# Attention with the values as the stationary operand, in two parts, and with weights that are divided before they move

## The chip, the cores and the metric

One core of a Trainium2 chip runs the whole program. The metric is device microseconds of one launch; lower is better. TensorE (PE) multiplies, VectorE (DVE), ScalarE (ACT) and GpSimd (POOL) do the rest, SyncE (SP) issues nearly all DMAs.

## The reference

Two blocks of two layers each work on 512 tokens of width 1024, in float32. Besides the attention there are a linear recurrence, cross-attention, two MLPs, a gated delta rule and two mixtures of experts; they stay as they are. The four attentions that the change rewrites are all of this form, with heads of 64 columns:

```python
for blk in range(s_len // BLOCK):          # blocks of 128 queries
    sc = einsum("bqhd,bkhd->bhqk", q[:, q0:q1], k[:, :q1]) * scale
    p = softmax(where(mask, sc + bias, -inf), axis=-1)
    outs.append(einsum("bhqk,bkhd->bqhd", p, v[:, :q1]))
```

- "fox" (`ab`, 8 heads, causal, a bias per head and key),
- "dilated" (`cd`, 8 heads, causal, a bias by distance),
- "sliding" (`cd`, 8 query heads on 2 key heads, a window of 128, and one sink logit per head that enters the denominator alone),
- "nsa" (16 heads, three branches whose outputs are added with a gate per head and branch: attention to 31 compressed blocks, and two causal attentions).

## The kernel before

The kernel is written with a tile framework: pools of buffers with a tag and a count (`BUFS`, `BANKS`), engines named by hand, and a scheduler that orders each engine's instructions when the program is built, by a simulated time and by program order as priority. So matmuls of a later projection stand between those of an attention, as filler. On the chip each engine then works in that fixed order. A later tile of a tag waits until an earlier one is released.

Precise products are made of rounded parts ("F32R"): `split` (L106) writes the rounded high part on ACT and the rest on DVE, and `mm3` (L148) adds three products.

The causal attentions run pair by pair (two heads, e = 0 and 1) through `j` in 8 steps: query block 3, 2, 1, 0, both heads of each. One step:

- `probs` (L289): two matmuls (three in fox) of `nk` = 512, 384, 256 or 128 columns into a bank "s"; DVE takes the minimum of the far columns (L301) and of the masked near ones (L302); ACT writes P = exp to SBUF, and the sum as `den` (L304).
- `pv` (L307): each 128 columns of P are transposed by PE into a bank "o" (L312), copied to SBUF as PT by `copy` (L776; ACT and DVE take turns, L781 and L783), and multiplied (L316) with PT as the stationary operand and 64 columns of the values as the moving one, both plain float32, into a bank "pt".

One head of a causal attention ("a unit" below: one head in one branch) so has 10 blocks of 128 keys: 10 transposes and 10 products. There are 8 units each in fox and dilated, 32 in nsa; sliding has 8 smaller ones, of 7 blocks. Per pair, `o_norm` (L318) divides by the sums on DVE, and `pair_out` (L326) transposes the result by four more matmuls (L332) and splits it into `ys`. In nsa (`branch` L1733, `compressed` L1696, `gated` L1767), the three branch outputs of a step `c` (8 steps, a pair each) are scaled and added in `acc` by DVE (L1777, L1775) and POOL (L1779), then go through `pair_out`.

The residual `hT` (4 tiles of tag "h") stays in SBUF through `ab` and `cd`. In nsa, four tiles of tag "y" hold the bias strips, `z` of `out_moe` (L1127, L1129) is of tag "h" in layer 1, and the first half of the output projection there (L1151) already runs in nsa's second half.

Of the kernel before, what the change touches and what calls it, by code (L numbers as in the profile page):

```python
# [18 lines left out]
S = 512  # L19
# [14 lines left out]
class Kern:  # L34
# [235 lines left out]
    def k_parts(self, y, name="K", tag="x"):  # L270


        nc = self.nc
        K, L = self.pair(name, tag, F32R), self.pair("KL", tag, F32R)
# [14 lines left out]
    def probs(self, qk, nk, strip, mn, den, extra=None, floor=None):  # L289
# [7 lines left out]
        P = self.t("P", tag="P")  # L297
# [6 lines left out]
        nc.scalar.activation(P[:, :nk], p[:, :nk], AF.Exp, bias=mn, scale=-1.0, accum_out=den)  # L304
        return P
# [12 lines left out]
    def o_norm(self, o, den, heads):  # L318
# [5 lines left out]
        return ob  # L324

# [38 lines left out]
    def ab(self):  # L364
# [8 lines left out]
        v = self.tiles("v", 4, "x")  # L373
# [5 lines left out]
        def ev_v(c, t, p):  # L379
            nc.scalar.activation(v[t][:, c * 256:(c + 1) * 256], p, AF.Copy, scale=rms()[0][:, t:t + 1])  # L380
# [47 lines left out]
        def attend(i):  # L428
            mn, den = self.small((128, 8), "mn"), self.small((128, 8), "den")
            o = self.psum("pt")  # L430
            for j in range(8):
                qb, e = NT - 1 - j // 2, j % 2
                h, nk, qs = 2 * i + e, (qb + 1) * 128, slice(qb * 128, (qb + 1) * 128)
                u = 8 * qb + h
                P = self.probs(self.qk(*parts[i], e, qs, slice(0, nk)), nk, self.fstrip, mn[:, j:j + 1], den[:, j:j + 1],
                               extra=(at[:, u:u + 1].to_broadcast([128, 128]), crh[:, :nk]))
                self.pv(o[:, j * 64:(j + 1) * 64], P, nk, [v[b][:, h * 64:(h + 1) * 64] for b in range(qb + 1)])
            ys[4 + i] = self.pair("y", "y", F32R)
            self.pair_out(self.o_norm(o, den, 8), ys[4 + i])
# [3 lines left out]
        for i in range(4):  # L443
# [6 lines left out]
            attend(i)  # L450
        ys[:4] = [self.rpair("y") for _ in range(4)]
# [71 lines left out]
    def cd(self):  # L523
        nc, V = self.nc, VCOL
        xs, rms = self.rms_prep(self.hT, V["cd_norm"])
        C, Sn = self.pair("CS")
# [12 lines left out]
        v = self.tiles("v", 4, "x")  # L539
        vd_ = self.t("vd")  # L540
        vd = [vd_[:, t * 128:(t + 1) * 128] for t in range(NT)]

        def ev_v(c, t, p):
            nc.scalar.activation(v[t][:, c * 256:(c + 1) * 256] if c < 2 else vd[t], p, AF.Copy, scale=rms()[0][:, t:t + 1])
# [18 lines left out]
        def dilated(i):  # L563
            mn, den = self.small((128, 8), "mn"), self.small((128, 8), "den")
            o = self.psum("pt")
            for j in range(8):
                qb, e = NT - 1 - j // 2, j % 2
                h, nk, qs = 2 * i + e, (qb + 1) * 128, slice(qb * 128, (qb + 1) * 128)
                P = self.probs(self.qk(qp[i], *kp[i], e, qs, slice(0, nk)), nk, self.dstrip[:, 512 - nk:],
                               mn[:, j:j + 1], den[:, j:j + 1])  # L570
                self.pv(o[:, j * 64:(j + 1) * 64], P, nk, [v[b][:, h * 64:(h + 1) * 64] for b in range(qb + 1)])
            self.pair_out(self.o_norm(o, den, 8), ys[i])

        def sliding(i):

            mn, den = self.small((128, 8), "mn"), self.small((128, 8), "den")
            o = self.psum("pt")
            for j in range(8):
                qb, e = NT - 1 - j // 2, j % 2
                h, k0, qs = i + 4 * e, max(0, qb - 1) * 128, slice(qb * 128, (qb + 1) * 128)  # L580
                nk = (qb + 1) * 128 - k0
                P = self.probs(self.qk(qp[4 + i], *kp[4], e, qs, slice(k0, k0 + nk)), nk, self.sstrip[:, 256 - nk:],
                               mn[:, j:j + 1], den[:, j:j + 1], floor=self.nsink[:, h:h + 1])
                self.pv(o[:, j * 64:(j + 1) * 64], P, nk,
                        [vd[k0 // 128 + b][:, e * 64:e * 64 + 64] for b in range(nk // 128)])
            x = self.small((128, 8), "es")
            sinks = self.nsink.rearrange("p (e i) -> p i e", e=2)[:, i]
            nc.vector.tensor_tensor(x.rearrange("p (t e) -> p t e", e=2), mn.rearrange("p (t e) -> p t e", e=2),
                                    sinks[:, None].to_broadcast([128, NT, 2]), op=OP.subtract)
            nc.scalar.activation(x, x, AF.Exp)  # L590
            nc.vector.tensor_tensor(den, den, x, op=OP.add)
            ys.append(self.rpair("y"))
            self.pair_out(self.o_norm(o, den, 8), ys[4 + i])
# [11 lines left out]
        for i in range(8):  # L605
# [5 lines left out]
            (dilated if i < 4 else sliding)(i % 4)  # L611
        for j in range(8):
# [605 lines left out]
    def ln_out(self, z, layer, out, y, ohT, w):  # L1218
# [9 lines left out]
        def add(t):  # L1228
# [11 lines left out]
            Rs[t] = self.T("R", "h" if layer == 0 else "y")  # L1240
# [64 lines left out]
    def moe(self, layer, lg, Rs, z, gain, parts):  # L1305
# [68 lines left out]
        oh = self.one_hot(0, pos3, iota, "h" if layer == 0 else "y")  # L1374
        begun = [self.gather(Rs, oh, r) for r in range(2)]
        space = self.all_space("h" if layer == 0 else "y")
# [45 lines left out]
        for i in range(0, 16, 2):  # L1422
# [4 lines left out]
            oh = self.one_hot(i + 2, pos3, iota, "h" if layer == 0 else "y")  # L1427
# [203 lines left out]
    def strips_load(self):  # L1631

        nc = self.nc
        st = [self.T("strip") for _ in range(4)]
        for i in range(4):
            src = self.skew[i][:]
            nc.sync.dma_start(st[i].rearrange("p (h n) -> p h n", h=4),
                              bass.AP(src.tensor, src.offset + 127, [[383, 128], [128 * 384, 4], [1, 256]]))
        self.strips = [st[h // 4][:, (h % 4) * 256:(h % 4 + 1) * 256] for h in range(16)]
        CB = self.T("CB")[:, :896]  # L1640
        nc.sync.dma_start(CB, self.cbd)
        self.CB = CB.rearrange("p (h i) -> p h i", h=16)

    def nsa(self):
# [3 lines left out]
        VV = [self.pair("vv", "x") for _ in range(2)]  # L1648
        wv = [list(wv(0)), list(wv(1, "x"))]
        for t in range(NT):  # L1650
            for c in range(2):
                self.lin_1(wv[c], t, xs, lambda p: self.copy(VV[t // 2][t % 2][:, c * 256:(c + 1) * 256], p))
# [21 lines left out]
        qp = [None] * 8  # L1674

        def proj_k(j):
# [3 lines left out]
            def ev(n, p):  # L1680
                kk[(n - 4) // 2] = self.k_parts(p, "K", "hx"[j])
# [4 lines left out]
        def proj_q(c):  # L1686
            def ev(n, p):
                qp[c] = self.q_parts(p, scale=-0.125)
            self.lin_f(w, [8 + c], xs, ev)
# [6 lines left out]
        def compressed(c):  # L1696
# [22 lines left out]
            return L_, r  # L1719

        def compressed_out(c, L, r, acc):
            pt = self.psum("o")
            for i in range(2):
                nc.tensor.transpose(pt[:, i * 128:(i + 1) * 128], L[:, i * 128:(i + 1) * 128], self.ident)
# [314 lines left out]
```

## Time and profile before

| | |
|---|---|
| median of 3 runs | 2849.57 us (2845.95 to 2852.29) |
| the profiled execution | 2845.23 us, of it the span 2843.4 us |
| fox, in the span | 125 to 200 us |
| dilated | 819 to 896 us |
| sliding | 896 to 995 us |
| nsa | 2278 to 2515 us |

The bounds of the four stages are those of their P and PT instructions, to a few microseconds; filler of the neighbours lies in them. A window's row gives, for each engine, the time in which it had an instruction under way. Matmuls overlap each other, so the price of one is read from the distance of starts in a dense run, not from its duration.

### The profile page before, as it was taken

To read this page: it belongs to the slowest core of one execution; us is meant where nothing else is said; L and a number is where in the kernel's file an instruction comes from. 1 tells how busy PE (TensorE), PEld (TensorE's weight loads), DVE (VectorE), ACT (ScalarE), POOL (GpSimd) and SP (SyncE) were. 2 spreads that over 40 slices of the span, in tenths; PEclk is the share of its full clock that TensorE was granted. 3 is DMA by queue.
4 is the path that set the end of the run, shared out by engine and by line. 5 is a ranking of instruction groups with operands and counts; after the bars stand their busy time and mean duration, and the time that the engine had idled before them with its cause. 6 is when DMAs were issued, how large, how long until landed. Compare 5 with 4: busy or idle time off the path is not lost. (4 is left out here: it accounts for less than half of the span.)

```text
span 2843.4 us, 40163 instructions
## 1 busy us (share of the span) xinstructions
PE 2695.0 (95%) x15128; PEld 2302.5 (81%) x15128; DVE 1769.7 (62%) x3583; ACT 1363.5 (48%) x2541; POOL 182.0 (6%) x185
## 2 busy tenths in 40 slices
PE   8999999999999999999999999979987999997995
PEld 6889888888888988888887888978776888896874
DVE  7675564444457655545446777668668377678767
ACT  5654442333356534422245444327774355535774
POOL 1101010000111010100001000000001011000001
PEclk9999999999999999999999999999998999998998
DMA  4314233333232421335333222327886211014885
GB/s 135 99 51 142 62 101 97 97 96 97 89 89 82 130 78 49 117 98 164 109 90 127 69 62 63 113 62 232 269 272 214 80 32 67 16 46 141 264 263 213
DMA packets 122535, 332.60 MB, mean 117 GB/s; under 512 B 21716, under 2 KB 37748, under 8 KB 122328
## 3 DMA queue, kind: packets, MB, share of 16 engines
q1 hardware_dynamic: 119896, 321.43, 36.1%
q0 software_dynamic: 2432, 8.46, 0.8%
q8 instruction: 124, 2.03, 0.3%
q14 instruction: 83, 0.68, 0.1%
HBM read 301.49 MB, written 28.02 MB: 116 GB/s over the span
## 5 line engine op out<-in xcount | busy, mean ns | idle before, releaser
L130 ACT ACTIVATE wh<-ws 128x1024 fp32r<-128x1024 f32 (+2 forms) x521 | 534.0, 1030 | 897.9 <-PE lin L152 599.5
L131 DVE TENSOR_TENSOR wl<-ws,wh 128x1024 fp32r<-128x1024 f32 (+2 forms) x521 | 617.0, 1191 | 221.6 <-ACT wh L130 220.6
L151 PE MATMUL lin<-xs,wh 128*128 128x512 f32 (+2 forms) x1080 | 429.0, 397 | 7.3 <-ACT xs L196 5.8
L152 PE MATMUL lin<-xs,wh 128*128 128x512 f32 (+2 forms) x1080 | 429.6, 398 | 2.5 <-DVE xs L197 2.5
L153 PE MATMUL lin<-xs,wl 128*128 128x512 f32 (+2 forms) x1080 | 428.6, 397 | 0.9 <-DVE wl L131 0.9
L151 PEld LDWEIGHTS lin<-xs,wh 128*128 128x128 f32 (+2 forms) x1080 | 203.3, 188 | 50.7 <-ACT xs L196 6.4
L152 PEld LDWEIGHTS lin<-xs,wh 128*128 128x128 f32 (+2 forms) x1080 | 203.2, 188 | 47.5 <-DVE xs L197 6.6
L153 PEld LDWEIGHTS lin<-xs,wl 128*128 128x128 f32 (+2 forms) x1080 | 203.3, 188 | 42.5 <-DVE wl L131 1.4
L346 DVE TENSOR_TENSOR h<-lin,h 128x512 f32<-128x512 f32 x112 | 77.4, 691 | 247.7 <-PE lin L153 247.5
L153 PE MATMUL lin<-sr,wl 128*128 128x512 f32 x512 | 199.3, 389 | 0.0
L152 PE MATMUL lin<-sr,wh 128*128 128x512 f32 x512 | 199.3, 389 | 0.0
L151 PE MATMUL lin<-sr,wh 128*128 128x512 f32 x512 | 199.2, 389 | 0.0
L733 DVE SCALAR_TENSOR_TENSOR ra<-lin,bc 128x512 f32<-128x512 f32 x64 | 44.2, 691 | 168.5 <-PE lin L153 165.9
L1535 PE MATMUL o<-oh,Rl 128*128 128x256 f32 x512 | 132.6, 290 | 7.2 <-PEq L1378 7.2
L304 ACT ACTIVATE P<-s,mn 128x256 f32<-128x256 f32 (+1 forms) x224 | 114.2, 514 | 52.7 <-DVE mn L302 50.0
L1535 PE MATMUL o<-oh,Rh 128*128 128x256 f32 x512 | 133.7, 293 | 4.9 <-issue 2.2
L152 PE MATMUL s<-wl,exh 128*128 128x512 f32 x256 | 107.4, 420 | 13.1 <-DVE wl L131 13.1
L151 PE MATMUL s<-wh,exh 128*128 128x512 f32 x256 | 103.0, 405 | 10.1 <-ACT wh L130 10.0
L152 PEld LDWEIGHTS lin<-sr,wh 128*128 128x128 f32 x512 | 96.1, 188 | 20.0
L151 PEld LDWEIGHTS lin<-sr,wh 128*128 128x128 f32 x512 | 96.1, 188 | 20.0
L153 PEld LDWEIGHTS lin<-sr,wl 128*128 128x128 f32 x512 | 96.1, 188 | 19.8
L1535 PEld LDWEIGHTS o<-oh,Rl 128*128 128x128 f32 x512 | 101.3, 198 | 13.3 <-issue 10.1
(605 smaller groups left out, 6178.4 us busy)
## 6 DMA issues: line engine op xcount, KB each, us to landing
ws<-in_moe_wgu SPq DMA_DIRECT2D x128, 512.0 KB, 4.9
ws<-in_mlp_wu SPq DMA_DIRECT2D x64, 512.0 KB, 3.6
ws<-in_mlp_wd SPq DMA_DIRECT2D x64, 512.0 KB, 3.6
ws<-in_moe_wd SPq DMA_DIRECT2D x64, 512.0 KB, 5.5
yd<-ey SPq DMA_DIRECT2D x56, 256.0 KB, 2.8
ws<-in_gdn_w SPq DMA_DIRECT2D x24, 512.0 KB, 3.6
ws<-in_ab_w SPq DMA_DIRECT2D x16, 512.0 KB, 4.3
ws<-in_xa_wk SPq DMA_DIRECT2D x16, 512.0 KB, 3.7
```

The lines of the kernel that those rows point to most:

```text
L130: nc.scalar.activation(wh, ws, AF.Copy)
L131: nc.vector.tensor_tensor(wl, ws, rd(wh), op=OP.subtract)
L151: mm(out, a[0], b[0], start=start, stop=False)
L152: mm(out, a[0], b[1], start=False, stop=False)
L153: mm(out, a[1], b[0], start=False, stop=stop)
L304: nc.scalar.activation(P[:, :nk], p[:, :nk], AF.Exp, bias=mn, scale=-1.0, accum_out=den)
L346: self.nc.vector.tensor_tensor(self.hT[n], p, self.hT[n], op=OP.add)
L733: nc.vector.scalar_tensor_tensor(a, p, 0.0, rms()[1], op0=OP.max, op1=OP.mult)
L1535: self.nc.tensor.matmul(p[:, j * 256:(j + 1) * 256], Rs[t][i][:, fs], oh[:, t], start=t + i == 0, stop=t == NT - 1 and i == 1)
```

## The change

1. The values are kept in two rounded parts side by side, 64 columns high and 64 low (`v_parts`: one ACT and one DVE instruction per evacuation instead of one on ACT). They take tiles "h" (fox, dilated), so `hT` is given up: it is loaded again from `xT` after fox; in `cd` it is stored to DRAM at the start and loaded after dilated.
2. `weigh`: the query blocks go two at a time, (2, 3), then (1, 0). One DVE reciprocal of two sums, then POOL multiplies each P by 1/sum and by a second scalar (ones, or nsa's gate), in SBUF. The two long P share a tile of 1024 columns.
3. `turn`: the transposes as before; their result is split (ACT and DVE, both) into two parts PT; for the long blocks these take tiles "wh" and "wl", which weights use too.
4. `causal`: the values (high and low columns) are the stationary operand, PT the moving one, 256 or 128 columns wide. 12 matmuls of a unit go into one bank "pt" (e = 0) or "lin" (e = 1). Its upper and lower 64 rows are added once (`head_out`: ACT copy, DVE add). The output is already transposed, so `pair_out` falls away.
5. In nsa all three branches add up in that bank, so `gated` falls away. The bias strips are loaded per step into "bc"; `z` and `Rs` of layer 1 change tags ("y" and "h").
6. Sliding: the sink logit is put as one more column behind the scores (a small ACT copy), in place of the three instructions on `es`.

```diff
-        nc.scalar.activation(P[:, :nk], p[:, :nk], AF.Exp, bias=mn, scale=-1.0, accum_out=den)
-        return P
+        n = nk
+        if sink is not None:
+            n += 1
+            nc.scalar.activation(p[:, nk:n], sink, AF.Copy)
+        nc.scalar.activation(P[:, :n], p[:, :n], AF.Exp, bias=mn, scale=-1.0, accum_out=den)
+        return P[:, :nk]
...
+    def weigh(self, qbs, probs, gate, tag):
+        wide = tag != "P"
+        x, den = self.t("P", tag=tag, cols=1024 if wide else 512), self.small((128, 2), "den")
+        Ps = [probs(qb, x[:, j * 512:] if wide else x[:, j * 257:], den[:, j:j + 1]) for j, qb in enumerate(qbs)]
+        r = self.small((128, 2), "rd")
+        self.nc.vector.reciprocal(r, den)
+        for j, P in enumerate(Ps):
+            self.nc.gpsimd.tensor_scalar(P, P, r[:, j:j + 1], gate(qbs[j]), op0=OP.mult, op1=OP.mult)
+        return Ps
+    def turn(self, Ps, PT):
+        p, n = self.psum("o"), 0
+        for P in Ps:
+            for b in range(P.shape[1] // 128):
+                self.nc.tensor.transpose(p[:, n * 128:(n + 1) * 128], P[:, b * 128:(b + 1) * 128], self.ident)
+                n += 1
+        self.split(p[:, :n * 128], *(x[:, :n * 128] for x in PT))
+    def causal(self, o, probs, V, gate, tag, first=True, last=True):
+        mm = self.nc.tensor.matmul
+        PT = self.turned()
+        for j, P in enumerate(self.weigh((2, 3), probs, gate, tag)):
+            self.turn([P], [x[:, j * 512:(j + 1) * 512] for x in PT])
+        for k, i in ((0, 0), (1, 0), (1, 1), (3, 0), (3, 1), (2, 0), (2, 1), (0, 1)):
+            x = PT[i].rearrange("p (q c) -> p q c", q=2)[:, k // 3:, k * 128:(k + 1) * 128]
+            mm(o[:, 256 + k // 3 * 128:], V(k), x, start=first and k + i == 0, stop=False)
+        PT = [self.t("PT", F32R, "PT") for _ in range(2)]
+        self.turn(self.weigh((1, 0), probs, gate, "P")[::-1], PT)
+        for k, i in ((0, 0), (1, 0), (1, 1), (0, 1)):
+            mm(o[:, k * 128:256], V(k), PT[i][:, k * 256:256 + k * 128], start=False, stop=last and (k, i) == (0, 1))
+    def head_out(self, e, o, y):
+        u = self.t("oh")[:64]
+        self.nc.scalar.activation(u, o[64:], AF.Copy)
+        self.nc.vector.tensor_tensor(y[e * 64:e * 64 + 64], o[:64], u, op=OP.add)
...
-        z = [self.T("z", "y" if layer == 0 else "h") for _ in range(NT)]
+        z = [self.T("z", "y") for _ in range(NT)]
...
         for c in range(8):
-            acc = self.t("acc", tag="bc")
-            L, r = compressed(c)
-            branch(c, 0, acc)
...
+            y = self.t("ob")
+            for e in range(2):
+                o = self.psum(("pt", "lin")[e])
+                nc.tensor.matmul(o, BD[:, c // 4 * 2 + e], PT, start=True, stop=False)
+                for br in range(2):
+                    branch(c, br, e, o)
+                    if c < 7 and e == 0:
+                        if br:
+                            PTn = compressed(c + 1)
+                        else:
+                            if c == 3:
+                                proj_k(1)
+                            proj_q(c + 1)
+                self.head_out(e, o, y)
```

## Rows read from the trace of the kernel before

**Rows 1.** The page, part 1: busy time of each engine over the span.
```profile
PE 2695.0 (95%) x15128; PEld 2302.5 (81%) x15128; DVE 1769.7 (62%) x3583; ACT 1363.5 (48%) x2541; POOL 182.0 (6%) x185
```

**Rows 2.** Busy time by windows: fox, dilated, sliding, nsa (us, engines, clock, DMA).
```profile
125.00:200.00 75.00, 70.05 (x455) 61.12 (x454) 57.75 (x168) 48.60 (x123) 8.76 (x11) 0.98 0.14 40
819.00:896.00 77.00, 76.75 (x480) 66.52 (x480) 57.04 (x131) 52.06 (x122) 15.51 (x14) 1.00 0.27 73
896.00:995.00 99.00, 95.25 (x701) 88.41 (x700) 68.25 (x160) 56.40 (x138) 3.83 (x3) 0.97 0.40 120
2278.00:2515.00 237.00, 228.53 (x1659) 206.04 (x1658) 172.43 (x582) 132.25 (x374) 24.98 (x42) 0.99 0.11 37
```

**Rows 3.** Waits of PE in nsa: total us, times, longest.
```profile
PE o L312 <- ACT P L304: 5.3, 3, 3.1
```

**Rows 4.** Matmuls by line: records, ns min/median/max, first and last start.
```profile
L316 PE MATMUL pt<-vv,PT x640: 217/275/422, 2282.9 to 2511.9; 128*128 128x64 f32 x160
L316 PE MATMUL pt<-v,PT x320: 217/275/324, 132.2 to 895.5; 128*128 128x64 f32 x160
...
L316 PE MATMUL pt<-vd,PT x112: 217/275/475, 899.0 to 992.6; 128*128 128x64 f32 x112
...
L332 PE MATMUL o<-c_ident,ob x48: 270/273/421, 143.2 to 994.2; 128*128 128x128 f32 x48
```

**Rows 5.** Timeline of PE in fox: start us, merged us, line, tile, columns, count.
```profile
165.16 0.61 PE L332 MATMUL o<-c_ident,ob 128*128 128x128 f32 x4
...
182.05 2.67 PE L316 MATMUL pt<-v,PT 128*128 128x64 f32 x22
...
187.03 0.27 PE L296 MATMUL s<-KL,Q 128*128 128x128 f32 x1
187.14 0.27 PE L296 MATMUL s<-crh,at 128*128 128x128 f32 x1
...
190.36 0.28 PE L151 MATMUL lin<-mx,wh 128*128 128x256 f32 x1
190.48 0.28 PE L152 MATMUL lin<-mx,wh 128*128 128x256 f32 x1
```

**Rows 6.** Groups by line in nsa, DVE then ACT: busy us, mean ns of one.
```profile
L1775 DVE SCALAR_TENSOR_TENSOR acc<-pt,rg,acc 128x64 f32<-128x64 f32 x64 | 13.0, 276 | 2.1 <-PE pt L316 2.0
...
L783 DVE COPY PT<-o 128x512 f32<-128x512 f32 x16 | 11.0, 687 | 3.9 <-PE o L312 3.8
...
L783 DVE COPY PT<-o 128x384 f32<-128x384 f32 x16 | 8.9, 557 | 13.9 <-PE o L312 13.8
...
L783 DVE COPY PT<-o 128x256 f32<-128x256 f32 x16 | 6.8, 424 | 14.0 <-PE o L312 12.6 <-PE s L296 1.2
...
L1777 DVE TENSOR_TENSOR acc<-pt,rg 128x512 f32<-128x512 f32 x8 | 5.5, 691 | 0.9 <-PE pt L316 0.4
...
L783 DVE COPY PT<-o 128x128 f32<-128x128 f32 x16 | 4.6, 289 | 5.2 <-PE o L312 4.9
...
L1745 DVE RECIPROCAL rg<-den 128x8 f32<-128x8 f32 x16 | 3.2, 201 | 5.4 <-ACT P L304 5.2
...
L781 ACT ACTIVATE PT<-o 128x512 f32<-128x512 f32 x16 | 9.6, 597 | 2.8 <-PE o L312 2.5
```

**Rows 7.** Groups of POOL by line, whole span: busy us, mean ns of one.
```profile
L206 POOL TENSOR_TENSOR ssq<-ssq,sq 128x512 f32<-128x512 f32 x42 | 69.2, 1649 | 110.1 <-ACT sq L201 90.7 <-issue 19.2
...
L277 POOL MEMSET KL<- 64x512 f32 x26 | 13.5, 520 | 116.9 <-PE pt L1818 90.6 <-PE s L296 25.1
...
L1779 POOL TENSOR_TENSOR acc<-acc,gtmp 128x512 f32<-128x512 f32 x8 | 10.2, 1280 | 114.0 <-DVE gtmp L1777 114.0
```

**Rows 8.** Timeline of PE at the end of fox: two waits of transposes.
```profile
175.64 0.66 PE L312 MATMUL o<-c_ident,P 128*128 128x128 f32 x4 [1.81 <-ACT P L304]
...
177.83 1.01 PE L312 MATMUL o<-c_ident,P 128*128 128x128 f32 x4 [1.01 <-ACT P L304]
```

**Rows 9.** Timeline of SP in nsa: the last two loads of z.
```profile
2391.01 0.79 SPq L1129 DMA_DIRECT2D z<-rdram  x2
```

More of the change, by code (lines that the diff above doesn't have):

```diff
@@ L273, in k_parts @@
         nc = self.nc
-        K, L = self.pair(name, tag, F32R), self.pair("KL", tag, F32R)
+        K, L = self.pair(name, tag[0], F32R), self.pair("KL", tag[-1], F32R)
         for e in range(2):
@@ new lines, in turn, with turned @@
+    def turn(self, Ps, PT):
[5 more added lines that the diff above has]
+        self.split(p[:, :n * 128], *(x[:, :n * 128] for x in PT))
+    def turned(self):
+        self.uid += 1
+        return [self.wp.tile([128, 1024], F32R, tag=tag, name=f"PT{tag}_{self.uid}", bufs=BUFS[tag]) for tag in ("wh", "wl")]
@@ L372, in ab @@
         u, g = self.tiles("u", 4), []
-        v = self.tiles("v", 4, "x")
+        v = [self.T("v", "h", F32R) for _ in range(NT)]
         def ev(n, p):
@@ L450, in ab @@
             attend(i)
+        self.hT = self.tiles("h", 8, "h")
+        for k in range(8):
+            nc.sync.dma_start(self.hT[k], A["xT"][k])
         ys[:4] = [self.rpair("y") for _ in range(4)]
@@ L525, in cd @@
         xs, rms = self.rms_prep(self.hT, V["cd_norm"])
+        hd = self.dp.tile([1024, S], F32, tag="hd", name="hd")
+        for k in range(8):
+            nc.sync.dma_start(hd[k * 128:(k + 1) * 128], self.hT[k])
         C, Sn = self.pair("CS")
@@ L572, in dilated @@
-            self.pair_out(self.o_norm(o, den, 8), ys[i])
-        def sliding(i):
[L576 to L591, printed above, removed]
@@ new lines, in dilated, with probs @@
+            y = self.t("ob")
+            for e in range(2):
+                h, o = 2 * i + e, self.psum(("pt", "lin")[e])
+                def probs(qb, P, den):
+                    nk = (qb + 1) * 128
+                    return self.probs(self.qk(qp[i], *kp[i], e, slice(nk - 128, nk), slice(0, nk)), nk,
+                                      self.dstrip[:, 512 - nk:], self.small((128, 1), "mn"), den, P=P[:, :nk])
+                self.causal(o, probs, lambda b: v[b][:, h * 128:(h + 1) * 128], lambda qb: self.ones[:, 0:1], "y")
+                self.head_out(e, o, y)
@@ L592, in sliding @@
             ys.append(self.rpair("y"))
-            self.pair_out(self.o_norm(o, den, 8), ys[4 + i])
+            self.split(y, *ys[4 + i])
         def proj(i):
@@ L611, in cd @@
             (dilated if i < 4 else sliding)(i % 4)
+            if i == 3:
+                self.hT = self.tiles("h", 8, "h")
+                for k in range(8):
+                    nc.sync.dma_start(self.hT[k], hd[k * 128:(k + 1) * 128])
         for j in range(8):
@@ L1718, in compressed @@
             nc.gpsimd.tensor_tensor(r8(r), r8(r), gates(c, 0), op=OP.mult)
[L1719 to L1724, printed above, removed]
-            PT = self.t("PTc", tag="PT")[:, :256]
-            self.copy(PT, pt[:, :256])
-            o = self.psum("pt")
-            for i in range(NT):
-                nc.tensor.matmul(o[:, i * 128:(i + 1) * 128], PT[:, i // 2 * 128:(i // 2 + 1) * 128],
-                                 BD[:, i % 2, c // 4 * 128:(c // 4 + 1) * 128], start=True, stop=True)
-            self.gated(acc, o, r, False)
```

171 lines of the change are left out of this document (91 added, 80 removed).

## The prediction

> **What bounds the kernel now.** I read the page's busy shares first: TensorE is under way in 95% of the span [rows 1], so a saving must be matmul time or a gap between matmuls. Then the windows of the four stages that the change touches, 488 us together [rows 2]: PE is busy 70.05 of 75, 76.75 of 77, 95.25 of 99 and 228.53 of 237 us, DVE only 0.77, 0.74, 0.69 and 0.73 of the time, ACT less. In nsa, the longest, PE's largest wait is 5.3 us in total [rows 3]. So PE bounds these stages, and the projections that lie in them as filler keep it full. Where filler runs out it shows: at the end of fox, transposes wait 1.81 and 1.01 us for the exponentials [rows 8].
>
> Next, what a matmul costs, by the distance of starts in dense runs [rows 5]. 22 records of the product P·V start over 2.67 − 0.28 us, 0.114 us each. Their number is the point of the change: 640 + 320 + 112 = 1072 records [rows 4], while the code has 10 products per causal unit (48 units) and 7 per sliding unit (8 units), 536 in all. A float32 product thus runs as two records, 0.228 us for 64 columns. Products of rounded parts are one record each: 0.12 us for 256 columns (190.36 to 190.48), 0.11 for 128 (187.03 to 187.14). Transposes start (0.61 − 0.27)/3 = 0.113 us apart.
>
> **The change, part by part.**
>
> *PE.* A causal unit pays 20 × 0.114 = 2.28 us for P·V now. After, it has 8 matmuls of 256 columns and 4 of 128: 8 × 0.12 + 4 × 0.11 = 1.40. That is −0.88, times 48 = −42.2 us. A sliding unit: 14 × 0.114 = 1.60 against 6 × 0.12 + 2 × 0.11 = 0.94, times 8 = −5.3. `pair_out` goes: 20 pairs of 4 transposes (48 of the 80 in [rows 4]), 80 × 0.113 = −9.0. In nsa's compressed branch 2 transposes and 8 records become 4 transposes and two matmuls of 512 columns (twice the 256-column price): 1.14 to 0.93 per step, times 8 = −1.7. Scores and transposes of P stay. The sum is −58 us: fox −8.8, dilated −8.8, sliding −7.1, nsa −33.5.
>
> *DVE.* A unit's four copies of PT are shared with ACT now: (687 + 557 + 424 + 289)/2 = 0.98 us on DVE [rows 6]. After, each goes through both engines, in three pieces of 512, 384 and 384 columns: 0.687 + 2 × 0.557 = 1.80. Two reciprocals at 0.20 come on top: +1.22 us per unit. A pair gains two adds of `head_out` at 0.69 (as a 512-column copy) and loses the product of `o_norm` (0.69, as L1777) and one reciprocal. Fox and dilated: 2 × 1.22 + 1.38 − 0.89 = +2.9 per pair, +11.7 us per stage. Sliding, by the same prices with pieces of 512 and 384 columns and without the `es` steps: +1.8 per pair, +7. Nsa, per step: 4 × 1.22 + 1.38 + some 0.5 for the compressed split, less 1.62 (L1775, 13.0 us in eight steps), two products of L1777 (1.38) and four small steps (0.8): +3.0, +24 us. DVE then carries 69.4 us in fox, 68.7 in dilated, 75.5 in sliding, 196 in nsa, where PE alone would leave 66, 68, 92 and 204. So DVE is late next, in fox and dilated at once. *ACT* gains about as much per unit (0.6 for 512 columns, [rows 6]), but starts from 132 of 237 in nsa, and stays below DVE. The second part of the values costs DVE a step per evacuation in the projections, beside PE's work; nothing for that, at most 1 us where it delays a bank.
>
> *The waits added.* Between exponential and transpose there are now a reciprocal (0.20) and POOL's scaling. No row shows POOL with one tensor and two scalars. The nearest: a memset, 0.52 us for 512 columns, and two tensors of 512 columns, 1.28 and 1.65 [rows 7]. I take 0.9, nearer the memset as one tensor is read; bounds 0.5 and 1.65. Behind a copy there is now ACT and then DVE (+0.6). A phase (two query blocks) so gains 1.8 to 4 us of latency, hidden while other phases or filler feed PE. POOL's throughput is no bound: 1280 columns in four units of a step cost 5 to 16.5 us against some 26.
>
> The Trainium skill speaks against this choice: "GPSIMD Engine Reference", section "Engine selection", sends elementwise work on a tile to VectorE, since GpSimd is about twice as slow with two inputs, though near line rate with one. The trace agrees on two inputs (1.28 us against DVE's 0.69); with one, no row shows it. By the slow reading the latency takes its upper end, by the other its lower; the PE sum is the same.
>
> *Moved loads.* `hT` comes back by eight loads after fox and after dilated; `ab_wo` needs it only after the cross-attention's key and value projections, `cd_wo` after sliding: hidden. The stores in `cd` end during the first projection. On SP they queue behind the release of the values' tiles, and weights stand behind them; four weight buffers cover that, 0 to 5 us, taken as 1. In nsa `z` was loaded by 2391 us [rows 9], 120 us ahead of the end, so half of the output projection could be filler. After, `z` shares tag "y" with PT's sources, values' keys and `ys`, and its four loads must wait for the last units: the filler goes, and the end of the stage drains bare. Fox loses filler too, since "lin" and "wh"/"wl" now also serve attention. I price an uncovered end like the waits of [rows 8], 2.8 us, three times, +1 for the loads: +9 us in total, bounds 2 and 20.
>
> *The sum.* If PE stayed the bound: −58 + 9. If DVE is, a stage takes its DVE time over the share that DVE can be kept busy. The trace has 0.77 as the highest share here (DVE not the bound) and 0.96 for PE (the bound, nsa). I take 0.92, nearer the latter, since the engine that bounds is the one kept fed: fox 69.4/0.92 = 75.4 (0), dilated 74.7 (−2), nsa 213 (−24), sliding by PE 92 (−7). That is −33 + 9 = −24 us. The profiled execution took 2845.2 us, 4 us below the median of the runs; the forecast is for the median, so 2849.6 − 24 = 2826.
>
> **The rivals.**
>
> 1. *DVE cannot be fed* (slower). Every step of a phase crosses engines, and DVE works in a fixed order. With a share f the causal stages take 334/f, sliding 92, the ends 9; with f = 0.86 that is the old 488 us. So below 0.86 the kernel gets slower; at 0.82 it is 407 + 92 + 9 − 488 = +20: 2870. For it: 0.77 is the most these stages show. Against: it was never the bound there, and PE reaches 0.96.
> 2. *POOL's latency takes the gain* (no change). 112 phases that each leave PE idle 0.2 to 0.3 us cost 24 to 34 us: about 2850. For it: POOL prices at two inputs, and only two or three buffers for P and PT. Against: nsa has three "s" banks and filler in seven of eight steps.
> 3. *PE stays the bound throughout*: −58 + 9, 2800; at the lower bound of the ends 2793. For it: DVE durations overlap in part, so its sums are too high.
> 4. *The products still run as two records*. Then only 11 us of PE are saved and DVE's load remains: about 2865. Rows of rounded parts show single records [rows 5], so hardly.
>
> **How the numbers follow.** My forecast with 3 as its lower edge (2797 to 2841): 0.66. Rival 1: 0.21; rival 2: 0.10; rival 4: 0.03. The range of 8 in 10 goes from 2797 to 2866, up to the milder half of rival 1. A difference of 0.2% (5.7 us) is about what a measurement of this kernel can tell from no change. Faster: 0.66 and 0.04 of rival 2, 0.70. Same: 0.08 with the rest of rival 2 and the edge of rival 1. Slower: 0.22.
>
> **What would show it.** Right: the P·V matmuls of the three stages number 12 and 8 per unit, single records 0.11 to 0.12 us apart; L332's transposes are gone; nsa is some 15 to 30 us shorter with DVE's share at 0.85 or more; fox and dilated hardly change; PE's waits in nsa name DVE, POOL or ACT, and the last step drains longer. Wrong: a DVE share in nsa that stays near 0.75 with PE's share falling (rivals 1 and 2: which engine PE waits for tells them apart, and POOL's duration at 512 columns whether it is POOL), or a long gap behind nsa or ahead of `ab_wo` or `cd_wo`, where a load came late.

## The result, and the profile after

| | before | after |
|---|---|---|
| median (4 runs each) | 2849.53 us | 2993.06 us (2986.13 to 2994.28) |
| ratio, 95% interval | | 1.0501 (1.0481 to 1.0521) |
| span of the profiled execution | 2843.4 us | 2990.9 us |

The change costs 5%. The page of the kernel after, part 1 (busy time, share of the span, instructions; before in [rows 1]):

```profile
PE 2745.8 (92%) x14584; PEld 2312.5 (77%) x14584; DVE 1831.2 (61%) x3671; ACT 1432.9 (48%) x2677; POOL 320.8 (11%) x409
```

TensorE issues fewer matmuls, 14584 for 15128, and is busy longer. The windows of fox, dilated, sliding, nsa, and of the output projection behind nsa, which answer to [rows 2] (columns as there: length, PE, PEld, DVE, ACT, POOL busy, granted clock, DMA):

```profile
126.00:214.00 88.00, 69.46 (x351) 55.55 (x352) 58.97 (x174) 52.01 (x126) 26.58 (x41) 0.87 0.08 25
844.00:947.00 103.00, 80.03 (x360) 63.99 (x359) 61.95 (x146) 56.70 (x127) 36.29 (x44) 0.81 0.18 49
950.00:1073.00 123.00, 105.33 (x642) 93.86 (x641) 74.59 (x165) 67.41 (x172) 23.82 (x36) 0.83 0.38 114
2353.00:2646.00 293.00, 242.48 (x1267) 197.47 (x1268) 187.71 (x580) 161.55 (x425) 98.00 (x171) 0.87 0.10 30
2647.00:2707.00 60.00, 57.98 (x469) 56.50 (x468) 39.62 (x102) 18.32 (x21) 0.53 (x6) 0.98 0.30 97
```

The four windows last 607 us; those of [rows 2] last 488. No engine is full: PE is under way in 0.83 of nsa, DVE in 0.64. Before, PE was idle in 8.5 us of nsa, now in 50.5. And the granted clock, 0.97 to 1.00 in the four windows before, is 0.81 to 0.87: PE now spends a part of each stage at the lower of its two levels, 1.2 instead of 2.4 GHz; in nsa the granted 0.87 means the lower level for 0.26 of 293 us, some 76 us, for some 5 before. PE's largest waits in nsa (for [rows 3]), and two waits of ACT and DVE there (us in total, times, longest):

```profile
PE s L296 <- ACT P L307: 22.2, 25, 2.8
PE o L1812 <- DVE Lp L108: 7.7, 8, 1.2
PE o L348 <- POOL P L340: 4.5, 9, 2.1
ACT Q L263 <- PE lin L153: 27.0, 7, 6.5
DVE Q L267 <- ACT Q L263: 28.6, 7, 6.5
```

PE waits most for a score bank that an exponential still holds, hardly for GpSimd. ACT and DVE stand 27 and 28.6 us behind seven query projections, where before they waited 0.4 and 0.3 us. A part of one step of nsa shows how it looks, first as four windows:

```profile
2429.50:2433.50 4.00, 3.18 (x24) 2.61 (x22) 1.83 (x4) 1.52 (x3) 0.00 (x0) 1.00 0.00 0
2433.50:2436.40 2.90, 0.14 (x1) 0.00 (x0) 1.38 (x2) 1.95 (x5) 0.00 (x0) 1.00 0.00 0
2437.00:2443.00 6.00, 5.68 (x28) 4.50 (x29) 3.70 (x13) 4.26 (x12) 2.41 (x4) 0.72 0.01 4
2443.00:2449.00 6.00, 6.00 (x30) 4.66 (x29) 1.89 (x8) 1.25 (x6) 2.41 (x4) 1.00 0.29 89
```

PE's instructions around the gap in it (timeline: start, length, idle time before and what ended it):

```profile
2432.79 0.85 PE L370 MATMUL lin<-PT,vv 128*128 128x128 f32 x3
2436.40 0.33 PE L296 MATMUL s<-K,Q 128*128 128x128 f32 x1 [2.76 <-ACT P L307]
2436.57 0.28 PE L296 MATMUL s<-KL,Q 128*128 128x128 f32 x1
...
2438.19 1.87 PE L348 MATMUL o<-c_ident,P 128*128 128x128 f32 x7
```

A head's last products end, and PE stands 2.76 us until an exponential frees a bank. The clock falls. The next head's chains start at half speed (28 matmuls in 6 us). Then the whole query projection, 24 matmuls, runs in one block with only two products of attention in it, at full clock, while ACT and DVE do little. A gap need not be that long: four of the twelve falls of the clock in nsa come behind a gap of 2.76 us, most of the others behind several of 0.4 to 0.8 us each (at 2420.2 us, for one, behind 0.40, 0.83, 0.36 and 0.60).

Call an unbroken run of projection matmuls in PE's order a group. By the trace, those of nsa stand in 78 groups before and in 17 after, the longest of 68; in fox 21 groups become 3, in dilated 38 become 9. Before, they filled the attention's gaps; after, attention and projection take turns.

**What the prediction counted, in the trace.** Products of nsa for one output bank (groups by form: duration min/median/max in ns, first and last start), for [rows 4]:

```profile
L366 PE MATMUL pt<-PTwh,vv x64: 220/330/522, 2365.7 to 2635.7; 128*128 128x256 f32 x48, 128*128 128x128 f32 x16
L370 PE MATMUL pt<-PT,vv x64: 221/283/337, 2367.6 to 2636.7; 128*128 128x256 f32 x32, 128*128 128x128 f32 x32
```

Starts in a dense run of them (timeline), for [rows 5]:

```profile
2431.87 0.39 PE L366 MATMUL lin<-PTwl,vv 128*128 128x256 f32 x1
2432.09 0.23 PE L366 MATMUL lin<-PTwh,vv 128*128 128x128 f32 x1
2432.15 0.27 PE L366 MATMUL lin<-PTwl,vv 128*128 128x128 f32 x1
2432.26 0.33 PE L366 MATMUL lin<-PTwh,vv 128*128 128x256 f32 x1
2432.43 0.40 PE L366 MATMUL lin<-PTwl,vv 128*128 128x256 f32 x2
2432.67 0.97 PE L370 MATMUL lin<-PT,vv 128*128 128x256 f32 x4
```

With the low parts and the other bank that is 12 single records per unit, 384 in nsa for 640. L332's transposes are gone.

### The profile page after: what moved, and what is told of

The parts are those of the page before. It is cut to its first block, busy times and chain, and to the rows that moved or that the text cites. A ratio compares the mean times of both kernels' runs of the same rounds, so it can differ in the third digit from the quotient of the medians.

```text
span 2990.9 us, 39635 instructions
## 1 busy us (share of the span) xinstructions
PE 2745.8 (92%) x14584; PEld 2312.5 (77%) x14584; DVE 1831.2 (61%) x3671; ACT 1432.9 (48%) x2677; POOL 320.8 (11%) x409
## 5 line engine op out<-in xcount | busy, mean ns | idle before, releaser
L296 PE MATMUL s<-K,Q 128*128 128x384 f32 (+1 forms) x224 | 94.2, 422 | 53.1 <-ACT P L307 47.2
L307 ACT ACTIVATE P<-s,mn 128x384 f32<-128x384 f32 (+1 forms) x224 | 114.3, 514 | 54.0 <-DVE mn L301 34.3
L348 PE MATMUL o<-c_ident,P 128*128 128x128 f32 x536 | 108.7, 337 | 29.1 <-POOL P L340 28.1
L348 PEld LDWEIGHTS o<-c_ident,P 128*128 128x128 f32 x536 | 77.0, 171 | 51.4 <-POOL P L340 43.5
L151 PEld LDWEIGHTS lin<-sr,wh 128*128 128x128 f32 x512 | 96.1, 188 | 20.0
```

What stands on the lines that cost most here:

```text
L151: mm(out, a[0], b[0], start=start, stop=False)
L296: nc.tensor.matmul(p[:, :nk], q, k, start=i == 0, stop=i == len(qk) - 1)
L307: nc.scalar.activation(P[:, :n], p[:, :n], AF.Exp, bias=mn, scale=-1.0, accum_out=den)
L348: self.nc.tensor.transpose(p[:, n * 128:(n + 1) * 128], P[:, b * 128:(b + 1) * 128], self.ident)
```

## Experiments

To read a stage alike in all kernels I take its time from its first minimum step on VectorE to the next event: fox to the first residual add of its output projection, dilated to sliding's first minimum, sliding to the first residual add of its output projection, nsa to the last matmul of its output projection. The kernel before, run beside them, took 2847.06 (e1 to e4), 2857.76 (e5 to e8), 2854.09 (e9 to e12), 2853.61 (e13 to e16), 2852.89 and 2851.76 us. Each changed kernel below was run once, so a difference of some 10 us means nothing. Each edit is also scheduled anew, so the order of every engine's instructions can change with it. Only e16 has the order of the kernel before in all engines; e7, e13 and e14, which add one or two instructions to it, do not.

| kernel | total | fox | dilated | sliding | nsa | sum of four |
|---|---|---|---|---|---|---|
| before | 2849.5 | 123 | 77 | 101 | 281 | 582 |
| after | 2993.1 | 151 | 107 | 134 | 354 | 746 |
| e1 scaling on VectorE | 2995.6 | 149 | 106 | 132 | 365 | 752 |
| e2 no division | (4383.7) | 142 | 94 | 128 | 341 | 705 |
| e3 long blocks one by one | 2987.4 | 144 | 107 | 144 | 344 | 739 |
| e4 lin free | 2988.3 | 153 | 104 | 134 | 356 | 747 |
| e5 scores ahead | 2992.7 | 151 | 103 | 138 | 354 | 746 |
| e6 fill | 3138.1 | 166 | 116 | 142 | 465 | 889 |
| e8 heads in turn | 3063.5 | 159 | 116 | 132 | 413 | 820 |
| e9 weights early | 2987.1 | 150 | 107 | 137 | 351 | 745 |
| e10 one copy | 2972.0 | 148 | 103 | 131 | 343 | 725 |
| e11 four weight buffers | 3192.0 | 158 | 100 | 135 | 353 | 746 |
| e15 chain as before | 2960.3 | 137 | 95 | 128 | 353 | 713 |
| e17 block products | 3036.1 | 150 | 109 | 124 | 399 | 782 |
| e18 filler free | 2920.1 | 136 | 94 | 124 | 315 | 669 |
| *on the kernel before:* e7 division | 2937.0 | 138 | 86 | 100 | 349 | 673 |
| e12 two weight buffers | 2893.1 | 130 | 79 | 103 | 287 | 599 |
| e13 GpSimd's step alone | 2875.9 | 129 | 91 | 99 | 298 | 617 |
| e14 reciprocal alone | 2894.8 | 131 | 79 | 100 | 321 | 631 |
| e16 single-part products | 2813.4 | 118 | 74 | 99 | 258 | 549 |

### One part of the change undone at a time: e1 to e5

```diff
e1  -  self.nc.gpsimd.tensor_scalar(P, P, r[:, j:j + 1], gate(qbs[j]), ...)
    +  self.nc.vector.tensor_scalar(P, P, r[:, j:j + 1], gate(qbs[j]), ...)
e2  -  self.nc.vector.reciprocal(r, den)     (and the scaling, in all stages)
e3  -  for j, P in enumerate(self.weigh((2, 3), probs, gate, tag)):
    -      self.turn([P], ...)
    +  for j, qb in enumerate((2, 3)):
    +      self.turn(self.weigh((qb,), probs, gate, "P"), ...)
e4  -  o = self.psum(("pt", "lin")[e])
    +  o = self.psum("pt")
e5  +  Ps, Qs = self.weigh((2, 3), probs, gate, tag), self.weigh((1, 0), probs, gate, "P")
       (both ahead of the first turn)
```

> The changed kernel with one edit: the scaling of P by 1/sum and the gate is done by VectorE in place of GpSimd; everything is computed as before. Theory A (the chain of one phase, scores to product, is too long, and GpSimd's two scalings of 0.52 to 0.77 us each with the hand-overs are its largest new link): VectorE takes about 0.35 to 0.6 us for each, so a phase gets some 0.6 us shorter and the kernel 20 to 40 us faster than the changed one (2993 us), if VectorE, at about 0.65 busy in these stages, has room. Rival B (the projections that served as filler are held back by the bank lin and by the weight buffers that attention now takes): no change within 10 us.

> The changed kernel without the reciprocal and without the scaling in the causal and sliding attentions: that part of the computation (division by the sums, and the gate of the two causal branches of nsa) is left out. It measures what the added links cost together. Theory A: 1.9 us less per phase, 112 phases, about two of them in flight: 80 to 110 us faster than the changed kernel, near or below 2900. Rival B: under 20 us.

> The changed kernel, but the two long query blocks go one at a time: each has its own reciprocal, scaling and tile P (tag P), so a block does not wait for the other's exponential, and the wide shared tile falls away. All is computed. Theory A: the first block's chain gets 1.5 us shorter, 20 to 50 us faster than the changed kernel. If the sharing of a tile and a reciprocal is harmless: within 10 us of it. Rival B: no change.

> The changed kernel, but both heads of a pair accumulate in the bank pt, one after the other, so that both banks lin are free for the projections again. All is computed. Rival B (the bank): the projections spread between the attention's matmuls again, 40 us or more faster than the changed kernel. Theory A: the projections gain nothing, and the second head has to wait for the first one's sum (1.3 us, 28 times): 0 to 40 us slower.

> The scores, sums and scaling of both phases of a head are put ahead of the first transposes in program order. Theory A (PE is starved because a head's phases follow one another, and the engines' fixed queues carry that order): the second phase's latency lies beside the first's, the four stages together lose at least 30 us, total 2960 or less, granted clock up. Rival B (what starves PE is the latency inside a phase and the three score banks, whichever phase stands first): within 12 us of the changed kernel, 2980 to 3005.

Of these only e2 moves, by 41 us of 164 in the four stages; its total says nothing, since with undivided values the first mixture of experts runs its overflow branch, 2048 matmuls that the kernel after does not issue. e1 takes GpSimd out of the chain, with a faster step (groups by form of L340 in nsa; ns, min/median/max), and gains nothing. The kernel after, on GpSimd:

```profile
L340 POOL TENSOR_SCALAR P<-P,rd,gt x128: 451/664/1170, 2357.2 to 2645.9; 128x384 f32<-128x384 f32 x32, 128x512 f32<-128x512 f32 x32, 128x256 f32<-128x256 f32 x32, 128x128 f32<-128x128 f32 x32
```

e1, on VectorE:

```profile
L340 DVE TENSOR_SCALAR P<-P,rd,gt x128: 331/475/827, 2347.8 to 2644.4; 128x384 f32<-128x384 f32 x32, 128x512 f32<-128x512 f32 x32, 128x256 f32<-128x256 f32 x32, 128x128 f32<-128x128 f32 x32
```

So the division in the chain costs, GpSimd's speed does not. e2's 41 us are half of what its theory asked for. The theory that one of these parts holds the rest falls.

### Can the gaps be filled? e6

```diff
+        for i in range(6):
+            self.nc.tensor.matmul(p[:, :128], self.identr, self.identr, start=True, stop=True)
         for P in Ps:      # turn: the transposes that overwrite p
```

> Ahead of the transposes of every phase, six matmuls of 128 columns without use are put into the bank that the transposes then overwrite: 160 such places x 6 x 0.11 us = 106 us of TensorE work more, at the full clock. Theory A (the idle gaps make the granted clock fall, and the lower clock then costs time by itself): the granted clock of the four stages rises from 0.79 to 0.87 towards 0.95 and the time does not rise, 2930 to 2995. Rival C (the clock is only a sign of the gaps, and costs nothing as PE has slack): the extra work shows in part or in full, 3010 to 3100.

It is 145 us slower than the kernel after, for some 106 us of work, and the clock stays low (0.80 in nsa). Both theories priced it too low. In the kernel after, PE waits only 4.5 us in nsa for GpSimd ahead of the transposes, and 22.2 ahead of the scores: the added matmuls stand mostly where PE would not have waited, and there they delay the chain. On the clock this run decides nothing.

### The division alone, in the kernel before: e7, e13, e14

```diff
         nc.scalar.activation(P[:, :nk], p[:, :nk], AF.Exp, ...)
e7  +  nc.vector.reciprocal(r, den)
e7  +  nc.gpsimd.tensor_scalar(P[:, :nk], P[:, :nk], r, self.ones[:, 0:1], op0=OP.mult, op1=OP.mult)
       (the division behind the products falls away; sliding is left as it was)
e13 +  nc.gpsimd.tensor_scalar(P[:, :nk], P[:, :nk], self.ones[:, 0:1], self.ones[:, 0:1], ...)
e14 +  nc.vector.reciprocal(self.small((128, 1), "rd"), den)
       (both in fox, dilated and nsa; the division stays where it was)
```

> The kernel before, with one part of the change alone: in fox, dilated and nsa each P is divided by its sum ahead of the transposes (a reciprocal on VectorE, the scaling on GpSimd); the values stay the moving operand and blocks come one by one, both heads in turn. Sliding is left as it was. Theory A1 (the division inside the chain is the main cost): fox, dilated and nsa rise by 70 us or more, total 2915 or more. Rival A2 (the division costs the 30 to 40 us that leaving it out gave back, or less, and the rest lies in the form of the products and the order of the heads): total 2847 to 2890.

> The kernel before, with GpSimd's step alone: in fox, dilated and nsa each P is multiplied by one twice on GpSimd, ahead of the transposes; no reciprocal, the division stays where it was. Scaling with the reciprocal cost this kernel some 85 us (2936.98). Theory A3 (the link itself, GpSimd's 0.5 to 0.8 us and the two hand-overs, is the cost): 2910 or more. Rival A4 (the reciprocal, which stands in VectorE's fixed queue and waits there for ScalarE's exponential, 26.8 us in nsa, is the cost): 2880 or less.

> The kernel before, with the reciprocal alone: in fox, dilated and nsa each block's sum gets a reciprocal on VectorE right behind its exponential, and nobody uses it. Nothing is added to the chain of a block, only to VectorE's queue. Theory A3 (the link): 2870 or less. Rival A4 (VectorE stands behind the exponential): 2900 or more.

e7 costs the kernel before 79 us, more than half of what the whole change costs. GpSimd's step alone costs 22, the unused reciprocal alone 41: A4 is nearer. Together they cost 79 for a sum of 63 by the totals, but 91 for 84 by the four stages, so whether they add up stays open. The window of nsa in e13:

```profile
2286.00:2538.00 252.00, 232.68 (x1644) 205.54 (x1642) 170.16 (x569) 129.88 (x371) 107.28 (x170) 0.99 0.10 35
```

In e14:

```profile
2282.00:2569.00 287.00, 265.35 (x1777) 233.38 (x1776) 197.55 (x721) 137.44 (x375) 26.02 (x42) 0.95 0.11 36
```

In e7:

```profile
2299.00:2610.00 311.00, 285.43 (x1762) 248.50 (x1761) 190.11 (x694) 134.15 (x373) 101.14 (x170) 0.88 0.10 33
```

What VectorE waits for at the reciprocal there (waits: us, times, longest), in e14:

```profile
DVE rd L306 <- ACT P L304: 36.1, 69, 1.8
```

In e7:

```profile
DVE rd L307 <- ACT P L304: 26.8, 38, 1.9
```

A reciprocal of one column takes 0.16 us, and nothing reads e14's. Its likely price is its place: VectorE works in a fixed order, stands in it until the exponential has ended, 36.1 us in nsa, and the next block's minimum and the next copy of PT stand behind it. Some of that replaces other waits: in these windows all waits of VectorE grow from 60 us before to 84. What the new orders of the other engines add to the 41 us was not tried apart. (The windows of e14 and e7 hold more of the output projection than that of before; their tails are shorter.)

### Buffers, split and order of heads: e8 to e12

```diff
e8   heads e = 0, 1 in turn, block by block, one reciprocal per block
e9  +  ws = list(w(9 + c)) if c < 7 else None     (start of a step of nsa)
    -  self.lin_f(w, [8 + c], xs, ev)
    +  self.lin_f((lambda n: ws) if ws else w, [8 + c], xs, ev)
e10 -  self.split(p[:, :n * 128], *(x[:, :n * 128] for x in PT))
    +  self.copy(PT[0][:, :n * 128], p[:, :n * 128])
e11 -  "ws": 4, "wh": 3, "wl": 3        (ws: the loads' staging buffers)
    +  "ws": 2, "wh": 4, "wl": 4
e12    (before) "wh": 2, "wl": 2
```

> The changed kernel with the two heads of a pair in turn, block by block, as the kernel before had them: each block has its own reciprocal and its own scaling, and the products of both heads come after both have been transposed; the products' number and form stay. If one head after the other is what starves PE: total 2900 or less, nsa (354 us with its projection) 320 or less. If the latency inside a block's chain or the missing filler is the cause: 2970 or more.

> The changed kernel; in nsa alone, the weights of the next step's query projection take their buffers, are loaded and split at the start of a step, ahead of the attention units, instead of behind the first unit. Theory B (the long weights PT share the three weight buffers wh and wl, so a projection's weights are split late, its 24 matmuls come as one block, and ScalarE and VectorE stand still behind the evacuation, 27.0 and 28.6 us in seven steps): these waits shrink, nsa falls from 354 us by 15 to 40. Theory A (the chains of the attention itself set the step): nsa within 8 us of 354.

> The changed kernel, in which the transposed weights are not split: one copy, by ScalarE and VectorE in turn as in the kernel before, is used in the place of both parts, with the weights halved by the scaling's second scalar; the low part of the weights is left out of the products, whose number stays. wl is then free for projections. If the split (two steps in a row, and 1.22 us more of VectorE per unit) is a main part of the loss: the four stages fall by 40 us or more in all, total 2950 or less. If not: by less than 15 us, 2978 or more.

> The changed kernel with four buffers wh and wl instead of three, at the price of two staging buffers ws instead of four (all stages with heavy weight loads may lose by that; read fox, dilated, sliding and nsa alone: 151, 107, 134, 354). Theory B (weight buffers): the four stages lose at least 25 us in all. Theory A: less than 10 us, or a rise.

> The kernel before with two buffers wh and wl instead of three, as if one were held by attention all the time. If weight buffers are what the change lacks: fox, dilated, sliding and nsa rise from 123, 77, 101 and 281 by 40 us or more in all. If not: less than 15 us in these stages, whatever the stages between them do.

The split is worth 21 us in the four stages, between the two bounds. Heads in turn make it worse (+74; this also doubles the reciprocals). e9 removes what I had taken for the cost: DVE's wait behind the query projection is 2.2 us, for 28.6, and the filler of nsa stands in 33 groups, for 17; yet nsa falls by 3 us. So that wait is a sign, and more groups alone do not help. Four weight buffers bring the four stages nothing (with half the staging buffers; outside them the kernel takes 199 us more), two cost the kernel before 17 us in them, little above the bound of 15: the count of buffers is hardly it either.

### Is TensorE's time worth anything? e16

```diff
-        PT = self.t("PT", tag="PT")
+        PT = self.t("PT", F32R, "PT")      # and the values as F32R tiles
```

> The kernel before, with its products P V in one rounded part: the transposed weights and the values are written rounded, and each product is one record of 64 columns instead of two. 536 records of 0.114 us fall away, 61 us of TensorE; no other instruction changes, and the low parts of weights and values are left out. If TensorE's work bounds these stages as the prediction took it: 2853 - 61 x 0.7 or more, 2790 to 2812. If those records filled time in which TensorE would have waited anyway: 2830 or more.

2813.4 us, 1 us above the range for a full PE; 40 less than the kernel beside it, for 61 us of matmuls less, and 33 less in the four stages. It leaves out the low parts, so it is a measurement and no offer. Its windows of fox and nsa:

```profile
127.00:196.00 69.00, 62.64 (x385) 52.51 (x384) 56.09 (x167) 46.93 (x122) 8.76 (x11) 0.98 0.14 47
2263.00:2475.00 212.00, 202.31 (x1321) 174.18 (x1319) 168.32 (x574) 129.46 (x372) 25.00 (x42) 0.97 0.12 41
```

PE stays under way in 0.95 of nsa, and DVE reaches 0.79. The order of all other work is that of before, in every engine. So PE did bound these stages, and with the chains and the filler of before the saved matmuls are worth half to two thirds of their time.

### What is left of it without division and split: e15, e17, e18

```diff
e15    e8 without reciprocal and scaling in fox, dilated, nsa, with e10's copy
e17 +  for qb in (3, 2, 1, 0):
    +      for o, probs, V, gate in heads:
    +          PT = self.t("PT", F32R, "PT")
    +          self.one(qb, probs, gate, [PT])
    +          for n in range(2 * qb + 2):
    +              k = n // 2
    +              self.nc.tensor.matmul(o[:, qb * 128:(qb + 1) * 128], V(k), PT[:, k * 128:(k + 1) * 128], ...)
e18    as e17, one head after the other, and
    -  o = self.psum(("pt", "lin")[e])
    +  o = self.psum("pt")
```

> The changed kernel with a chain like that of before: heads in turn, block by block; in fox, dilated and nsa no reciprocal and no scaling (the weights stay undivided, so these values are wrong, and what follows the attention routes differently: read fox, dilated, sliding and nsa alone), the transposed weights copied once, used for both parts. The values stay the stationary operand, 12 products per unit. If the loss sits in the division, the split and the order of the heads: fox, dilated and nsa fall to those of before or below (123, 77 and 281 at most, 480 in all, nsa without its 14 us of lost filler 270). If the form of the products itself does it (TensorE without dense work of its own, clock down): their sum stays above 530.

> The kernel of the run with the chain as before (no division in fox, dilated and nsa, one copy; these values are wrong, what follows routes differently: read the stages alone), in which each block's products follow its own transposes, 128 columns at a time and in the order of before (blocks 3 to 0, both heads in turn, one PT of 512 columns for each block): 20 products per unit instead of 12, 2.2 us of TensorE instead of 1.4. Sliding stays as in the changed kernel. If the products held back to the end of a phase (two blocks of a head, 8 products at once) are what starves PE: fox, dilated and nsa fall from 137, 95 and 353 (585 in all) to 510 or less in spite of the 40 us more of TensorE work. If it is what surrounds them (one bank per head held over a whole step, the filler and its order, the compressed branch): 570 or more.

> As the run with block products (no division in fox, dilated and nsa, one copy, 20 products per unit right behind their transposes; these values are wrong, read the stages alone), but both heads of a pair take their bank from pt, one head after the other, so that lin is left to the projections, while no PT of these three stages takes wh or wl. In the fixed order of TensorE the 216 or 203 projection matmuls of nsa then stand in 61 groups between attention instead of 26, as in the kernel before (59). Theory F (what starves TensorE is the filler: an attention that holds lin or wh and wl lets projections run only as one block, with ScalarE and VectorE standing still behind it, and bare attention in between; undoing one of the two alone does nothing): fox, dilated and nsa fall from 150, 109 and 399 (658) to 540 or less, granted clock in nsa from 0.78 to 0.9 or more. Rival G (the stationary values and the output held over a step, whatever the filler): 610 or more.

e15 has the chain of before and 12 product records per unit for 20, and its three stages still take 585 us for 481. e17 is slower still, 658, for some 40 us more of PE's work: holding the products back is not what starves PE. e18 does the same work as e17 and takes 545, 113 less, 5 above what theory F allowed and far below its rival. The window of nsa in e17:

```profile
2349.00:2692.00 343.00, 292.68 (x1552) 251.00 (x1552) 161.44 (x489) 148.48 (x396) 19.12 (x43) 0.78 0.09 29
```

PE's largest waits in it:

```profile
PE o L348 <- ACT P L307: 23.5, 9, 3.6
PE s L296 <- ACT P L307: 9.4, 18, 1.8
```

The window of nsa in e18:

```profile
2318.00:2583.00 265.00, 244.65 (x1598) 203.73 (x1598) 164.04 (x495) 146.60 (x396) 21.20 (x43) 0.99 0.12 40
```

PE's largest waits in it:

```profile
PE o L348 <- ACT P L307: 8.4, 16, 1.3
PE o L1813 <- DVE Lp L108: 4.0, 7, 1.1
```

The longest wait falls from 3.6 to 1.3 us, PE's idle time from 50 to 20 us, and the clock stays at 0.99. The projection matmuls stand in 74 groups in e18's trace and in 29 in e17's. What differs is that no attention bank comes from lin, and that a head's output bank is held for one head instead of two; the two were not tried apart, and heads in turn cost 74 us where the division stood between (e8). Neither e17 nor e18 takes wh and wl for PT in these stages. So neither wh and wl free with lin held (e17: 29 groups) nor lin free with wh and wl held (e4: 17 groups, as without it, and no gain) spreads the filler again; both free, with one head after the other, do (e18).

The filler's place is the likely cause of the 113 us, not shown by itself, and it is not the whole. The number of groups does not order the times: e7 has 114 in its window of nsa, and nsa still takes 349 us there. And e18, with no division, no split, the filler spread and nsa's clock back, still takes 545 us where the kernel before takes 481. Sliding, which keeps its division in e15, e17 and e18, stays at 124 or more in every variant of the changed kernel, for 101 before. What these 64 and 23 us are was not found; the form of the products itself stays a rival for them.

## Why the prediction was wrong

The forecast was 2826 us, with a range from 2797 to 2866; the kernel takes 2993.

- **TensorE bounds: right.** e16 shows it.
- **−58 us of matmuls: right in kind, somewhat too high.** 12 and 8 single records per unit, no L332. In the run shown, seven products start from 2431.87 to 2432.67 us, 0.13 us apart on average where I took 0.11 and 0.12, so a unit saves nearer 0.7 than 0.88 us. The stage was no longer limited by them.
- **"Hidden while other phases or filler feed PE": the step that failed.** I counted the latency that a phase gains, 1.8 to 4 us, and named its cover, but not what becomes of the cover. PE's idle time in nsa rose from 8.5 to 50.5 us. Two things were missed. First, the division sits in fixed queues: even with the products and the heads' order of before, where PE had been under way in 0.96 of nsa, it cost 79 us (e7). A reciprocal in VectorE's queue that nothing reads makes that kernel 41 us slower (e14); I had priced such an instruction at its 0.20 us. Second, the cover itself went: the output banks and the PT tiles come from lin, wh and wl, and the projections, which were the filler, became blocks between the heads (78 groups to 17). I saw the sharing and priced it only at the end of fox. e17 to e18 gives 113 us for lin together with the order of the heads, without the division, in a form that is not quite the changed kernel's. How the 144 us divide between the two stays open.
- **DVE is next at a share of 0.92: wrong.** Its load was below my sum (187.7 for 196 in nsa, 59.0 for 69.4 in fox), its share 0.60 to 0.67. Rival 1 had this form: with its own formula and a share of 0.64 it gives 334/0.64 + 92 + 9 − 488 = +135, 2985 us. That it comes so near is luck: it has the causal stages at 522 us for 484, sliding at 92 for 123 and the ends at 9 for 38. I priced it only down to 0.82, taking the 0.69 to 0.77 of [rows 2] as a floor; those were shares beside a full PE. And it named DVE, while what could not be fed were all engines; PE waits most for ACT (22.2 us in nsa).
- **GpSimd at 0.9 us: too high, and of no weight.** For 512 columns it takes 0.77 us; the middle of 128 over all widths is 0.664. PE waits 4.5 us for it in nsa, so rival 2 did not come either (its 112 phases at 0.2 us are 22 us, not 24), and e1 shows that its speed does not matter. As to the Trainium skill's preference for VectorE ("GPSIMD Engine Reference", section "Engine selection"): the same step is faster there, 0.475 us in e1 for the 0.664, and the time is the same.
- **Ends +9, at most 20: too low.** From the end of the window to the first residual add or the last matmul: fox 63 for 51, sliding 12 for 2, nsa 61 for 45, 38 us together. Fox and nsa lost the projections that had run inside the stage. 13 us came back between sliding and nsa; why was not tried.
- **The clock was left out.** It was at 0.87, 0.81, 0.83 and 0.87 in the four windows, for 0.98, 1.00, 0.97 and 0.99. If PE could have used all of that, it is 88 × 0.13 + 103 × 0.19 + 123 × 0.17 + 293 × 0.13 = 90 us, for 7 before: an upper bound, as PE also waits. In the rows of nsa this looks like PE being busy for 14 us more than before ([rows 2]), though the attention's matmuls are 33 us less by my count. The stretch shown above is one pattern: 2.76 us without a matmul, then half clock. "TensorE: Matmul & The Clock Gate" of the Trainium skill (Part 1) states that an idle array goes back to the lower rate. How much of the 144 us the clock costs by itself stays open: e18, which closed most gaps of nsa, also brought its clock back, to 0.99, and no run moved it alone.

Open too: the parts do not add. In the four stages division gives back 41 (e2) and the split 21 (e10) of 164, yet the division alone costs the kernel before 91 there (e7). A reading that fits, but was not shown: each of them is enough to open gaps, and taking one away leaves the others.

## What to carry to other kernels

A stage with one full engine and loose others is kept full by filler and by chains short enough for its few banks: before saving matmuls, ask which buffers and banks the new form takes, and whose filler lived in them. An instruction in a fixed queue can cost the time for which the engine must stand there, not its own duration; price a reciprocal behind another engine's exponential by what it holds up. Where a saving shortens the dense work and lengthens the chain, price idle gaps with the lower clock behind them.

## What the runs showed of the hardware

- GpSimd multiplies a tile by two per-row scalars in 0.77 us for 512 columns (mean of 32 in nsa), nearer the memset's 0.52 than the two-tensor 1.28 and 1.65 of [rows 7] (group by line, as there):

```profile
L340 POOL TENSOR_SCALAR P<-P,rd,gt 128x512 f32<-128x512 f32 x32 | 24.7, 772 | 0.0
```

- The gap of 2.76 us on PE that is shown above was followed by some 3.5 us at the 1.2 GHz level; seven transposes of 128 columns in it start 0.24 us apart on average, instead of 0.11. The clock also fell behind several gaps of 0.4 to 0.8 us, and PE's busy time in nsa rose while its work fell.
- A rounded product with 64 moving columns is one record too (e16); four of them end 0.63 us after the first start, as the timeline shows:

```profile
2292.80 0.63 PE L316 MATMUL pt<-vv,PT 128*128 128x64 f32 x4
```

That is (0.63 − 0.28)/3 = 0.12 us from start to start, with the 0.28 us that one lasts; the float32 product of the kernel before took two of 0.114 [rows 5].
